# Sixteen of the 22 k-tiles of an FFN output projection as seven products of quarters, with the weight sums made in scratch DRAM

## The chip, the core and the metric

The kernel runs on one core of one Trainium2 chip. A core has five engines, each with an instruction queue of its own: TensorE (PE, matmuls; its weight loads are listed as PEld), VectorE (DVE), ScalarE (ACT), GpSimd (POOL) and SyncE (SP, which here only issues transfers). Transfers run on 16 DMA engines; most are issued by SP, and those that add to what they write are issued by POOL. Matmuls write to PSUM, eight banks of 128 x 512 words; everything else works on SBUF. The metric is the device time of the whole program in microseconds: 1425.68 us before the change, the median of 3 runs (1422.99 to 1426.24).

## What is computed

A trunk of two layers on x (512 tokens x 1024), with 256 memory tokens. Each layer has a token mixer, cross-attention and a SwiGLU FFN, each followed by a residual and a layer norm. Cut to what matters here:

```python
D_MODEL, SEQ, DEPTH = 1024, 512, 2
D_FF = 2816                       # 22 k-tiles of 128

def swiglu(x, w_in, w_out):
    g, u = jnp.split(x @ w_in, 2, axis=-1)
    return (jax.nn.silu(g) * u) @ w_out

h = layer_norm(x, ln0_g, ln0_b)
for l in range(DEPTH):
    mix = hybrid_mixer(h, ...)
    h = layer_norm(DEEPNORM_ALPHA * h + mix, ln1_g[l], ln1_b[l])
    xa = memory_cross_attention(h, mem, w_xq[l], w_xkv[l], w_xo[l])
    h = layer_norm(DEEPNORM_ALPHA * h + xa, ln2_g[l], ln2_b[l])
    ff = swiglu(h, w_ffn_in[l], w_ffn_out[l])
    h = layer_norm(DEEPNORM_ALPHA * h + ff, ln3_g[l], ln3_b[l])
```

All data are float32.

## The kernel before

**Three matmuls for one.** A float32 operand is split into a high part, which ScalarE copies into the matmul's type (line 101), and a low part, which VectorE or POOL subtracts (line 102). A product is three matmuls: high x high, high x low, low x high (`mm3`, lines 138 to 141).

**Buffers.** A weight chunk of 128 x 1024 words (512 KB) is loaded by SP into one of four `raw` buffers, then split into one of four `ring` tiles or, if it has to stay, into a `block` (`wchunk`, lines 121 to 136; `split_quarter`, line 355). There are 15 blocks of 8 KB per partition for everything that is large. PSUM has four banks with the tag `acc`, two with `tr` and two with `cv`. A tile that is asked for waits until a buffer of its tag is free.

**Order.** The code is written as one program. A scheduler, working at compile time with a simulated timeline, takes for each engine the ready instruction that stands first in the program; blocks under `tc.high_priority` count as standing further ahead. What it chose is then fixed: on the chip each engine runs its list in that order and waits at semaphores.

**The stages of a layer.** Mixer, first output projection (`po_mo`), cross-attention (`xq`, `scores`, `attn_out`, output projection `po_xo`), layer norm, FFN (lines 914 to 934).

**The FFN's input.** `swiglu_seven` (line 385) makes two k-tiles of the FFN's hidden layer, a pair, from seven products of quarters instead of eight: the layer norm's output is held as four quarters and their sums (`Quads`, line 299); the sums of weight quarters are made by two VectorE additions (lines 397, 398) and two adding DMAs from POOL (`add_into`, line 295). Each product is 24 matmuls of 256 columns into a pair of banks X, W or Y. At the end of a pair VectorE multiplies the two 128 x 512 results (line 464) and splits them (line 465) into `ph` and `pl`. The first pair of each layer goes through `swiglu_plain` (line 361), eight products.

**The FFN's output.** The 22 k-tiles come in three parts of 8, 6 and 8. After each part `out_proj` (line 267) multiplies the hidden k-tiles (stationary) with rows of `w_ffn_out` (moving, 512 columns at a time) for the four token tiles, and VectorE adds each bank into the residual `h` (line 286). The last part also makes the layer norm of each token tile. Chunks 0 to 3 of the weights go into the ring, the others into blocks.

**Lines of the prediction besides these.** 482 (transposes of the memory tokens), 507, 516 and 517 (loads of x and of two rows of the first norm), 554 and 555 (POOL applies the first norm's gain and bias to h), 566 (load of the convolution's rows), 584 (POOL clears `attT` at the head of each layer), 172 (loads of a norm's gain and bias), 351 and 125 (loads of weights).

Of the kernel before, what the change touches and what calls it, by code (L numbers as in the profile page):

```python
# [20 lines left out]
P = 128  # L21
# [30 lines left out]
def trunk(ctx: ExitStack, tc, a, out):  # L52
# [20 lines left out]
    def block(shape, dt, name):  # L73
        return blk.tile(shape, dt, tag="b", name=name)
# [25 lines left out]
    def split(hi, lo, src, eng=DVE):  # L100
        ACT.activation(hi, src, AF.Copy)  # L101
        eng.tensor_sub(lo, src, f(hi))  # L102
# [191 lines left out]

    def add_into(dst, src):

        POOL.dma_start(dst, src, accum_op=ALU.add)  # L297

    class Quads:

# [57 lines left out]
        split(flat[:, 0], flat[:, 1], raw)  # L358
        return w

    def swiglu_plain(w, q, j, ph, pl, name):
# [13 lines left out]
        out = []  # L375
        with tc.high_priority(offset=HP):
            for m in range(2):
                sg = tmp.tile([P, T], F32, tag="t", name=f"sg{j}{m}_{name}")
                ACT.activation(sg, banks[0][m], AF.Silu)
                DVE.tensor_mul(sg, sg, banks[1][m])  # L380
                split(ph[:, m, :], pl[:, m, :], sg)
                out.append((ph[:, m, :], pl[:, m, :]))
        return out

    def swiglu_seven(w, q, j, ph, pl, i0, name):

# [22 lines left out]
        def product(wq, b, banks, start, stop):  # L409
            for m in range(2):  # L410
                ms = slice(m * P, (m + 1) * P)
                for k in range(4):
                    wh, wl, bh, bl = wq[:, 0, k, ms], wq[:, 1, k, ms], b[:, 0, k, :], b[:, 1, k, :]
                    o = banks[m][:, :256]
                    PE.matmul(o, wh, bh, start=start and k == 0, stop=False, skip_group_check=True)  # L415
                    PE.matmul(o, wh, bl, start=False, stop=False, skip_group_check=True)  # L416
                    PE.matmul(o, wl, bh, start=False, stop=stop and k == 3, skip_group_check=True)  # L417
# [36 lines left out]
        product(w3, q.b[1, 1], X, False, True)  # L454
        with tc.high_priority(offset=HP):
            for m in range(2):
                ACT.activation(sg[m][:, hi], X[m][:, lo], AF.Silu)
        product(w4, t4, W, False, True)
        out = []
        with tc.high_priority(offset=HP):  # L460
            for m in range(2):
                DVE.tensor_add(uu[m][:, lo], W[m][:, lo], u2[m])
            for m in range(2):
                DVE.scalar_tensor_tensor(sg[m], sg[m], -1.0, uu[m], ALU.mult, ALU.mult)
                split(ph[:, i0 + m, :], pl[:, i0 + m, :], sg[m])
                out.append((ph[:, i0 + m, :], pl[:, i0 + m, :]))
        return out


    def mem_T(name):  # L470
# [89 lines left out]
    for l in range(L):  # L560
# [324 lines left out]
        def attn_out(hd, PT):  # L885
            oh, ol = oT[hd // 2]
            for e in range(2):
                po = bank(n_(f"o{hd}{e}"), tag="cv" if hd == XH - 1 else "acc")
                es = slice(hd * 256 + e * P, hd * 256 + (e + 1) * P)
                for m in range(2):  # L890
                    mm3(po, V[0][:, m, es], V[1][:, m, es], PT[:, 0, m, :], PT[:, 1, m, :], m == 0, m == 1)
                i = (hd % 2) * 2 + e
                split(oh[:, i, :], ol[:, i, :], po)

        q0, q1 = xq((0, 1), halves=True)
# [16 lines left out]


        w_fi, w_fo = a["w_ffn_in"][l], a["w_ffn_out"][l]
        for part, (j0, nj) in enumerate(((0, 8), (8, 6), (14, 8))):
            pT = []
            for j in range(j0, j0 + nj, 2):
                if (j - j0) % 4 == 0:
                    ph = block([P, 4, T], F32R, n_(f"ph{j}"))
                    pl = block([P, 4, T], F32R, n_(f"pl{j}"))  # L920
                if j == 0:
                    pT += swiglu_plain(w_fi, quads, j, ph, pl, f"{l}")
                else:
                    pT += swiglu_seven(w_fi, quads, j, ph, pl, (j - j0) % 4, f"{l}")
            norm = None
            if part == 2:
                gb3 = load_gb(a["ln3_g"][l], a["ln3_b"][l], n_("ln3"))
                hT = new_hT(n_("ln3")) if l < L - 1 else None

                def norm(tt, st):  # L930
                    layer_norm(tt, st, gb3, n_("ln3"), hT,
                               store=out[0, tt * P:(tt + 1) * P, :] if l == L - 1 else None)
            out_proj(w_fo[j0 * P:(j0 + nj) * P, :], pT, n_(f"fo{part}"), ALPHA if part == 0 else 1.0, norm=norm,
                     fin=part == 2 and l == L - 1)


_NAMES = [
# [18 lines left out]
```

## Time and profile before

| | |
|---|---|
| median of 3 runs | 1425.68 us (1422.99 to 1426.24) |
| the profiled execution | 1427.96 us, its span from the first to the last instruction 1426.0 us |
| granted TensorE clock, mean | 0.996 |
| DMA | 168.63 MB, 118 GB/s on average |
| weight chunks of `w_ffn_out` | 44 loads of 512 KB by SP |
| adding DMAs | 40 of 512 KB by POOL, all SBUF to SBUF |
| first and last `po_fo` matmul of layer 0's three parts | 454.3 to 503.4, 558.3 to 596.5, 671.6 to 722.5 us |
| the same in layer 1 | 1150.1 to 1199.1, 1254.1 to 1292.3, 1367.4 to 1416.9 us |

The profile is one execution; times in it are counted from the first instruction. "Busy" is the time in which an engine has at least one instruction in work. TensorE's matmuls overlap, so their mean duration is longer than the distance from one to the next. The chain of work is followed back from the last instruction, at each step to what released it. A wait is put down to the event that came last before the instruction could start.

### The profile page before, as it was taken

What the parts mean: (1) busy time and instruction counts of PE and PEld (TensorE: products, weight loads), DVE (VectorE), ACT (ScalarE), POOL (GpSimd) and SP (SyncE); (2) the same over time, 40 slices, a digit from 0 to 9 for tenths busy, and PEclk for the clock granted to TensorE, in tenths of its full rate; (3) what the DMA queues carried; (4) which work ended last, traced back from release to release, by engine and by line L of the source; (5) the groups of instructions that cost most, each with busy time, mean ns of one, the idle gap of its engine ahead of it and who ended that gap; (6) DMA issues with size and microseconds to landing.
All of it is one profiled execution on the core that took longest, in us unless ns stands there. A gap on an engine that the chain in (4) does not pass through costs nothing.

```text
span 1426.0 us, 22119 instructions
## 1 busy us (share of the span) xinstructions
PE 1396.7 (98%) x8949; PEld 1251.3 (88%) x8949; DVE 1034.0 (73%) x1701; ACT 608.0 (43%) x977; POOL 151.4 (11%) x98
## 2 busy tenths in 40 slices
PE   7998989999999999999999999999999999999997
PEld 6787888988899899899897889889889998989996
DVE  6699978656886376576769999685678764756667
ACT  5552461442456055255136235524525632534540
POOL 2373330000010000000013200000000000000000
PEclk9999999999999999999999999999999999999999
DMA  7522242322265364465242235512215663545531
GB/s 253 152 63 90 86 151 71 105 70 92 75 163 148 104 155 126 122 167 155 77 124 89 74 114 168 163 59 89 78 42 142 165 181 75 137 144 134 163 104 60
DMA packets 109306, 168.63 MB, mean 118 GB/s; under 512 B 7548, under 2 KB 82000, under 8 KB 109204
## 3 DMA queue, kind: packets, MB, share of 16 engines
q1 hardware_dynamic: 103156, 145.99, 31.9%
q0 software_dynamic: 5760, 20.97, 7.8%
q8 instruction: 70, 1.15, 0.3%
q14 instruction: 32, 0.26, 0.1%
q10 hardware_dynamic: 288, 0.26, 0.1%
HBM read 144.13 MB, written 2.10 MB: 103 GB/s over the span
## 4 chain that ended last, share of the span: by engine, by line
PE 85%; DVE 6%; issue 3%; ACT 3%; POOL 2%; DMA 1%; SPq 0%; DVEq 0%; POOLq 0%; ACTq 0%
PE po_fo L140 6%; PE po_fo L139 6%; PE po_fo L141 6%; PE fx L417 5%; PE fx L415 5%; PE fx L416 5%; PE fw L416 3%; PE fw L417 3%; PE fw L415 3%; DVE cv L611 3%; PE pp_xq L139 2%; PE pp_xq L140 2%; PE pp_xq L141 2%; PE po_xo L141 2%; PE po_xo L139 2%
## 5 line engine op out<-in xcount | busy, mean ns | idle before, releaser
L611 DVE SCALAR_TENSOR_TENSOR cv<-u,chan,cv 128x511 f32<-128x511 f32 (+29 forms) x240 | 159.6, 728 | 0.2
L140 PE MATMUL po_fo<-w_fo,ph 128*128 128x512 f32 (+1 forms) x360 | 138.2, 385 | 0.0
L141 PE MATMUL po_fo<-w_fo,pl 128*128 128x512 f32 (+1 forms) x360 | 137.6, 385 | 0.0
L297 POOL DMA_DIRECT2D s<-raw_a x40 | 34.8, 873 | 952.9 <-PE pp_f L141 473.8
L139 PE MATMUL po_fo<-w_fo,ph 128*128 128x512 f32 (+1 forms) x360 | 132.0, 385 | 0.0
L101 ACT ACTIVATE w_a<-raw_a 128x1024 fp32r<-128x1024 f32 x60 | 63.2, 1055 | 135.6 <-PE po_fo L141 110.2
L102 DVE TENSOR_TENSOR w_s<-s,w_s 128x1024 fp32r<-128x1024 f32 x80 | 97.3, 1220 | 28.3 <-ACT w_s L101 28.1
L101 ACT ACTIVATE w_s<-s 128x1024 fp32r<-128x1024 f32 x80 | 83.8, 1053 | 46.6 <-DMA s<-raw_a 33.6
L286 DVE SCALAR_TENSOR_TENSOR h<-h,po_fo 128x512 f32<-128x512 f32 (+1 forms) x49 | 32.6, 674 | 90.6 <-PE po_fo L141 90.6
L417 PE MATMUL fx<-T_ln,w_s 128*128 128x256 f32 x320 | 90.6, 283 | 0.0
L416 PE MATMUL fx<-T_ln,w_s 128*128 128x256 f32 x320 | 90.6, 283 | 0.0
L415 PE MATMUL fx<-T_ln,w_s 128*128 128x256 f32 x320 | 90.6, 283 | 0.0
L102 DVE TENSOR_TENSOR w_a<-raw_a,w_a 128x1024 fp32r<-128x1024 f32 x60 | 73.2, 1220 | 11.7 <-ACT w_a L101 10.5
L141 PEld LDWEIGHTS po_fo<-w_fo,pl 128*128 128x128 f32 x360 | 67.7, 188 | 13.2
L140 PEld LDWEIGHTS po_fo<-w_fo,ph 128*128 128x128 f32 x360 | 67.7, 188 | 13.0
L139 PEld LDWEIGHTS po_fo<-w_fo,ph 128*128 128x128 f32 x360 | 67.3, 188 | 12.9
L102 DVE TENSOR_TENSOR w_fo<-raw_fo,w_fo 128x1024 fp32r<-128x1024 f32 x44 | 52.9, 1219 | 16.2 <-ACT w_fo L101 16.2
L415 PEld LDWEIGHTS fx<-T_ln,w_s 128*128 128x128 f32 x320 | 61.4, 192 | 0.0
L416 PEld LDWEIGHTS fx<-T_ln,w_s 128*128 128x128 f32 x320 | 61.4, 192 | 0.0
L417 PEld LDWEIGHTS fx<-T_ln,w_s 128*128 128x128 f32 x320 | 61.4, 192 | 0.0
L140 PE MATMUL pp_xq<-hT_ln,w_xq 128*128 128x256 f32 (+1 forms) x192 | 61.3, 322 | 0.0
L139 PE MATMUL pp_xq<-hT_ln,w_xq 128*128 128x256 f32 (+1 forms) x192 | 60.0, 320 | 0.5 <-ACT hT_ln L101 0.5
(317 smaller groups left out, 4420.5 us busy)
## 6 DMA issues: line engine op xcount, KB each, us to landing
raw_a<-w_ffn_in SPq DMA_DIRECT2D x60, 512.0 KB
raw_fo<-w_ffn_out SPq DMA_DIRECT2D x44, 512.0 KB
s<-raw_a POOLq DMA_DIRECT2D x40, 512.0 KB, 5.1
s<-w_ffn_in SPq DMA_DIRECT2D x20, 512.0 KB
raw_xv<-w_xkv SPq DMA_DIRECT2D x16, 512.0 KB
raw_c<-w_in SPq DMA_DIRECT2D x16, 512.0 KB
raw_xk<-w_xkv SPq DMA_DIRECT2D x16, 512.0 KB
raw_mo<-w_mix_out SPq DMA_DIRECT2D x16, 512.0 KB
```

The costliest lines, as they stand in the source:

```text
L101: ACT.activation(hi, src, AF.Copy)
L102: eng.tensor_sub(lo, src, f(hi))
L139: PE.matmul(o, lh, rh, start=start, stop=False)
L140: PE.matmul(o, lh, rl, start=False, stop=False)
L141: PE.matmul(o, ll, rh, start=False, stop=stop)
L286: DVE.scalar_tensor_tensor(h[tt][:, c0:c1], h[tt][:, c0:c1], scale, bks[c][:, :c1 - c0], ALU.mult, ALU.add)
L297: POOL.dma_start(dst, src, accum_op=ALU.add)
L415: PE.matmul(o, wh, bh, start=start and k == 0, stop=False, skip_group_check=True)
L416: PE.matmul(o, wh, bl, start=False, stop=False, skip_group_check=True)
L417: PE.matmul(o, wl, bh, start=False, stop=stop and k == 3, skip_group_check=True)
L611: DVE.scalar_tensor_tensor(cv[ct][:, s:], u[:, ct, :T - s], wj, cv[ct][:, s:], ALU.mult, ALU.add)
```

## The change

The parts are now of 8, 8 and 6 k-tiles. The output projections of the first two use `out_proj_seven`: the hidden tiles (2 halves of k by 2 halves of the tokens) and the weights (2 halves of k by 2 halves of the columns) are taken as quarters, and seven products of sums of quarters replace eight. k-tiles are paired even with odd, so each pair of the FFN's input gives one tile of each quarter. The sums of hidden quarters T1 to T4 are made by VectorE when a pair is ready (`PairQuads`), the sums of weight quarters S1 to S4 in scratch DRAM: SP copies a quarter there, and POOL adds the other terms by adding DMAs. The calls that issue these stand in the code of cross-attention, four steps (eight transfers) at a time. The third part stays with `out_proj`.

```diff
+    dram = ctx.enter_context(tc.tile_pool(name="dram", bufs=1, space=bass.MemoryType.DRAM))
...
-        POOL.dma_start(dst, src, accum_op=ALU.add)
+        POOL.dma_start(dst, src, accum_op=ALU.add, max_dma_last_dim=4096)
...
+    class PairQuads:
+        PLACE = {"11": (0, 4, 6, 10), "21": (1, 5, 7, 11), "22": (2, 3, 8, 9)}
+        SUMS = {"T1": 0, "T2": 1, "T4": 2, "T3": 3}
+
+        def __init__(self, j0, name):
+            self.j0 = j0
+            self.t = [block([P, 2, 4, 256], F32R, f"pT{i}_{name}") for i in range(4)]
+            self.b = [block([P, 2, 4, 256], F32R, f"pB{i}_{name}") for i in range(3)]
...
+        def second(self, j, sg, uu):
+            i = (j - self.j0) // 2
+            t3 = uu[1][:, 256:]
+            DVE.tensor_sub(t3, sg[1][:, 256:], sg[0][:, 256:])
+            split(*self.get("T3", i), t3)
+            split(*self.get("22", i), sg[1][:, 256:])
+
+        def first(self, j, sg, uu):
+            i = (j - self.j0) // 2
+            for m, n in enumerate(("11", "21")):
+                split(*self.get(n, i), sg[m][:, :256])
+            t1, t2, t4 = uu[0][:, :256], uu[0][:, 256:], uu[1][:, :256]
+            DVE.tensor_sub(t1, sg[0][:, :256], sg[0][:, 256:])
+            DVE.scalar_tensor_tensor(t2, t1, -1.0, sg[1][:, 256:], ALU.mult, ALU.subtract)
+            DVE.scalar_tensor_tensor(t4, t2, -1.0, sg[1][:, :256], ALU.mult, ALU.subtract)
+            split(self.t[i][:, 0, 0:2, :].rearrange("p e c -> p (e c)"),
+                  self.t[i][:, 1, 0:2, :].rearrange("p e c -> p (e c)"), uu[0])
+            split(*self.get("T4", i), t4)
+
+    def quarter_of(w, c, k, u):
+        v = w.rearrange("(q two p) c -> two p q c", two=2, p=P)
+        return v[k][:, 2 * u:2 * u + 2, c * 512:(c + 1) * 512]
+
+    def weight_sums(w, name):
+        s = {n: [dram.tile([P, 2, 512], F32, tag=f"{n}{u}_{name}", name=f"{n}{u}_{name}") for u in range(2)]
+             for n in ("S1", "S2", "S3", "S4")}
+        steps = []
+        for n, c, k in (("S3", 0, 0), ("S1", 1, 0), ("S2", 1, 1), ("S4", 0, 1)):
+            steps.append([lambda u=u, n=n, c=c, k=k: nc.sync.dma_start(s[n][u], quarter_of(w, c, k, u)) for u in range(2)])
+        for n, x in (("S3", (1, 0)), ("S1", (1, 1)), ("S2", "S3"), ("S4", "S2")):
+            steps.append([lambda u=u, n=n, x=x: add_into(s[n][u], s[x][u] if x in s else quarter_of(w, *x, u))
+                          for u in range(2)])
+        return s, steps
+
+    def out_proj_seven(w, sums, pq, name, scale):
...
+        def operand(n, u):
+            raw = stage.tile([P, 1024], F32, tag="raw", name=f"raw_{n}{u}_{name}")
+            src = sums[n][u] if n in sums else quarter_of(w, *A[n], u)
+            nc.sync.dma_start(raw.rearrange("p (k c) -> p k c", k=2), src)
+            wt = ring.tile([P, 2, 1024], F32R, tag="w", name=f"w_{n}{u}_{name}")
+            split(wt[:, 0, :], wt[:, 1, :], raw)
+            return wt
+
+        plan = (("S3", "T3", "W"), ("11", "11", "X"), ("12", "21", "Y"), ("S2", "T2", "X"), ("22", "T4", "W"),
+                ("S1", "T1", "X"), ("S4", "22", "X"))
+        tags = {"X": "acc", "W": "tr", "Y": "cv"}
...
+        def add(t, c, g, i):
...
+                DVE.scalar_tensor_tensor(h[tt][:, cs], h[tt][:, cs], k, banks[g][i], ALU.mult,
+                                         ALU.subtract if c else ALU.add)
...
+        for n, b, g in plan:
+            bank_major = n in ("S1", "S4")
+            parts = [(i, u) for i in range(2) for u in range(2)] if bank_major else \
+                [(i, u) for u in range(2) for i in range(2)]
+            for i, u in parts:
+                for k in range(2):
+                    ph, pl = pq.get(b, u * 2 + k)
...
+                    PE.matmul(o, ph[:, ts_], wh, start=first, stop=False, skip_group_check=True)
+                    PE.matmul(o, ph[:, ts_], wl, start=False, stop=False, skip_group_check=True)
+                    PE.matmul(o, pl[:, ts_], wh, start=False, stop=last, skip_group_check=True)
...
     def swiglu_seven(...)
...
+            if quads:
+                for m in range(2):
+                    DVE.scalar_tensor_tensor(sg[m][:, hi], sg[m][:, hi], -1.0, uu[m][:, hi], ALU.mult, ALU.mult)
+                dest.second(j, sg, uu)
         product(w4, t4, W, False, True)
...
-                DVE.scalar_tensor_tensor(sg[m], sg[m], -1.0, uu[m], ALU.mult, ALU.mult)
-                split(ph[:, i0 + m, :], pl[:, i0 + m, :], sg[m])
+                s = lo if quads else slice(0, T)
+                DVE.scalar_tensor_tensor(sg[m][:, s], sg[m][:, s], -1.0, uu[m][:, s], ALU.mult, ALU.mult)
+            dest.first(j, sg, uu)
...
+        sums = [weight_sums(a["w_ffn_out"][l][g * NK * P:(g + 1) * NK * P, :], n_(f"fs{g}")) for g in range(2)]
+        steps = [st for g in range(2) for st in sums[g][1]]
...
         q0, q1 = xq((0, 1), halves=True)
+        sum_step(4)
         pt0 = scores(0, q0)
         q2, = xq((2,))
+        sum_step(4)
         pt1 = scores(1, q1)
         attn_out(0, pt0)
+        sum_step(4)
         pt2 = scores(2, q2)
         q3, = xq((3,))
+        sum_step(4)
         pt3 = scores(3, q3)
...
-        for part, (j0, nj) in enumerate(((0, 8), (8, 6), (14, 8))):
+        for part, (j0, nj) in enumerate(((0, 8), (8, 8), (16, 6))):
+            seven = part < 2
+            p = PairQuads(j0, n_(f"p{part}")) if seven else Pairs(j0, nj, n_(f"p{part}"))
...
+            if seven:
+                out_proj_seven(w_part, sums[part][0], p, n_(f"fo{part}"), scale)
+                continue
```

Per layer that is 16 copies of 512 KB on SP's queue, 16 adding DMAs of 512 KB on POOL's, and 14 instead of 8 (or 6) weight chunks to load and split in each of the two projections.

More of the change, by code (lines that the diff above doesn't have):

```diff
@@ L374, in swiglu_plain @@
                                 kh == 0 and k == 0, kh == 1 and k == 3)
-        out = []
         with tc.high_priority(offset=HP):
+            sg, uu = ([tmp.tile([P, T], F32, tag="t", name=f"{s}{j}{m}_{name}") for m in range(2)] for s in ("sg", "uu"))
             for m in range(2):
[L378 to L382, printed above, removed]
@@ L383, in swiglu_plain, with __init__ @@
-        return out
-    def swiglu_seven(w, q, j, ph, pl, i0, name):
+                ACT.activation(sg[m], banks[0][m], AF.Silu)
+                DVE.tensor_mul(sg[m], sg[m], banks[1][m])
+            dest.second(j, sg, uu)
+            dest.first(j, sg, uu)
+    class Pairs:
+        def __init__(self, j0, nj, name):
+            self.j0 = j0
+            self.t = [[block([P, 4, T], F32R, f"p{j}{i}_{name}") for i in range(2)] for j in range(0, nj, 4)]
+            self.stat = [(self.t[i // 4][0][:, i % 4, :], self.t[i // 4][1][:, i % 4, :]) for i in range(nj)]
+        def second(self, j, sg, uu):
+            pass
+        def first(self, j, sg, uu):
+            for m in range(2):
+                split(*self.stat[j - self.j0 + m], sg[m])
@@ L389, in swiglu_seven @@
+    def swiglu_seven(w, q, j, dest, name):
         n = lambda s: f"{s}{j}_{name}"
@@ L457, in swiglu_seven @@
                 ACT.activation(sg[m][:, hi], X[m][:, lo], AF.Silu)
+            if quads:
+                for m in range(2):
+                    DVE.scalar_tensor_tensor(sg[m][:, hi], sg[m][:, hi], -1.0, uu[m][:, hi], ALU.mult, ALU.mult)
+                dest.second(j, sg, uu)
         product(w4, t4, W, False, True)
-        out = []
         with tc.high_priority(offset=HP):
@@ L914, in trunk, with norm @@
         w_fi, w_fo = a["w_ffn_in"][l], a["w_ffn_out"][l]
-        for part, (j0, nj) in enumerate(((0, 8), (8, 6), (14, 8))):
-            pT = []
+        for part, (j0, nj) in enumerate(((0, 8), (8, 8), (16, 6))):
+            seven = part < 2
+            p = PairQuads(j0, n_(f"p{part}")) if seven else Pairs(j0, nj, n_(f"p{part}"))
             for j in range(j0, j0 + nj, 2):
[L918 to L934, printed above, removed]
+                (swiglu_seven if j else swiglu_plain)(w_fi, quads, j, p, f"{l}")
+            scale = ALPHA if part == 0 else 1.0
+            w_part = w_fo[j0 * P:(j0 + nj) * P, :]
+            if seven:
+                out_proj_seven(w_part, sums[part][0], p, n_(f"fo{part}"), scale)
+                continue
+            gb3 = load_gb(a["ln3_g"][l], a["ln3_b"][l], n_("ln3"))
+            hT = new_hT(n_("ln3")) if l < L - 1 else None
+            def norm(tt, st):
+                layer_norm(tt, st, gb3, n_("ln3"), hT,
+                           store=out[0, tt * P:(tt + 1) * P, :] if l == L - 1 else None)
+            out_proj(w_part, p.stat, n_(f"fo{part}"), scale, norm=norm, fin=l == L - 1)
 _NAMES = [
```

42 lines of the change are left out of this document (39 added, 3 removed).

## The prediction

> **What bounds the kernel now.** I read the page's busy times and its chain of work first, then the windows, then rows of the timeline.
>
> ```profile
> span 1426.0 us, 22119 instructions
> PE 1396.7 (98%) x8949; PEld 1251.3 (88%) x8949; DVE 1034.0 (73%) x1701; ACT 608.0 (43%) x977; POOL 151.4 (11%) x98
> ...
> PE 85%; DVE 6%; issue 3%; ACT 3%; POOL 2%; DMA 1%; SPq 0%; DVEq 0%; POOLq 0%; ACTq 0%
> ```
>
> TensorE holds 85% of the chain that ended last. The windows say where it doesn't (columns: stretch, its length, busy time of PE, PEld, DVE, ACT and POOL with their instructions, granted clock, DMA share, GB/s):
>
> ```profile
> 0.00:10.00 10.00, 3.50 (x14) 2.95 (x15) 3.36 (x7) 3.63 (x5) 2.09 (x10) 1.00 0.77 259
> 10.00:39.00 29.00, 24.56 (x109) 19.36 (x109) 22.46 (x60) 18.30 (x22) 5.75 (x2) 1.00 0.66 232
> ...
> 255.00:374.00 119.00, 118.75 (x689) 104.17 (x688) 78.40 (x155) 44.63 (x85) 0.00 (x0) 1.00 0.24 78
> 374.00:454.00 80.00, 79.90 (x663) 79.27 (x662) 64.22 (x91) 44.63 (x72) 5.35 (x6) 1.00 0.55 146
> 454.00:504.00 50.00, 50.00 (x248) 42.46 (x247) 23.05 (x28) 13.19 (x16) 0.85 (x1) 1.00 0.41 122
> ```
>
> In layer 0 cross-attention runs from 255 to 374 us, and the FFN follows: products of its input projection to 454, then the output projection (`po_fo`) of the first part to 504. There TensorE has no gap at a granted clock of 1.00. The start is different: up to 39 us TensorE works 28 of 39 us, and the transfers are busy 0.77 and 0.66 of the time, the most of the whole span. A matmul that goes is therefore worth its full pace in the FFN, and DMA work that is harmless at 300 us isn't at 20 us.
>
> A busy matmul is not its pace, since matmuls overlap. The pace is the distance of starts, in rows of the timeline (start, duration):
>
> ```profile
> 484.10 0.39 PE L140 MATMUL po_fo<-w_fo,ph 128*128 128x512 f32 x1
> ...
> 490.22 0.39 PE L140 MATMUL po_fo<-w_fo,ph 128*128 128x512 f32 x1
> ...
> 442.77 0.28 PE L415 MATMUL fw<-T_ln,w_s 128*128 128x256 f32 x1
> ...
> 443.61 0.28 PE L416 MATMUL fw<-T_ln,w_s 128*128 128x256 f32 x1
> ```
>
> From 484.10 to 490.22 there are 27 steps: 0.2267 us per 512-wide matmul. From 442.77 to 443.61 there are 7: 0.120 us per 256-wide one.
>
> **What goes.** An output projection of 8 k-tiles takes 4 token tiles x 8 x 2 column halves x 3 = 192 matmuls of 512 columns. Seven products take 7 x 2 x 4 x 3 = 168. Two such parts in each of two layers save 4 x 24 = 96 matmuls; 8+8+6 k-tiles instead of 8+6+8 changes nothing else in the count but a few 256-wide matmuls of the last tile (under 0.1 us). 96 x 0.2267 = **21.8 us**. Nothing else is removed, so this is the most that can be gained.
>
> The Trainium skill's page "TensorE: Matmul & The Clock Gate", section "Back-to-back issue gap", gives a sustained spacing of about 131 ns for 512 columns beside the weight loads; by it the 96 would be worth 12.6 us. The trace disagrees with 226.7 ns, and the sum goes by the trace.
>
> **What is added to VectorE and ScalarE.** Durations (columns: shape, count, then total busy and mean ns):
>
> ```profile
> L102 DVE TENSOR_TENSOR w_s<-s,w_s 128x1024 fp32r<-128x1024 f32 x80 | 97.3, 1220 | 28.3 <-ACT w_s L101 28.1
> L102 DVE TENSOR_TENSOR pl<-sg,ph 128x512 fp32r<-128x512 f32 x44 | 30.1, 683 | 0.0
> L446 DVE TENSOR_TENSOR sg<-fy,x 128x256 f32<-128x256 f32 x40 | 16.8, 421 | 23.4 <-PE fy L417 23.4
> L286 DVE SCALAR_TENSOR_TENSOR h<-h,po_fo 128x512 f32<-128x512 f32 x47 | 31.8, 685 | 88.4 <-PE po_fo L141 88.4
> L101 ACT ACTIVATE w_fo<-raw_fo 128x1024 fp32r<-128x1024 f32 x44 | 45.9, 1054 | 18.0 <-DMA raw_fo<-w_ffn_out 15.7 <-PE fy L417 2.2
> ...
> 430.49 0.42 DVE L446 TENSOR_TENSOR sg<-fy,x 128x256 f32<-128x256 f32 x1
> 430.83 1.23 DVE L102 TENSOR_TENSOR w_a<-raw_a,w_a 128x1024 fp32r<-128x1024 f32 x1
> ```
>
> Per pair of k-tiles in the FFN's input, VectorE now does 9 x 1.22 (seven splits, two sums) + 6 x 0.42 + 4 x 0.683 = 16.2 us, against 7 products x 24 x 0.120 = 20.2 us of TensorE. The change replaces the last four instructions (2.7 us) by thirteen of 256 columns and one of 512 (13 x 0.42 + 0.68 = 6.1 us): 19.6 of 20.2 us. The last two rows, starts 0.34 us apart at a duration of 0.42, show that real occupancy is less. A seven-product output projection needs 14 weight splits and 14 adds into h: 14 x 1.22 + 14 x 0.685 = 26.7 us beside 168 x 0.2267 = 38.1 us of TensorE. A whole part: VectorE 4 x 19.6 + 26.7 = 105 of 4 x 20.2 + 38.1 = 119 us, 89%, before 65%. ScalarE gets 14 x 1.05 = 15 us in 38. Both fit on average, so I cost them at what isn't covered. (a) At the end of a pair VectorE's clump grows from 3.1 to 5.7 us. Four weight tiles in the ring are up to 4 x 2.88 = 11.5 us of products ahead, which hides it; I take 0.1 us in each of 16 pairs, 1.6 us. Uncovered it is 16 x 2.6 = 42 us; below nothing it can't be, as it adds work only. (b) The first product of each output projection needs T3 of the last pair, which is made one product (2.88 us) earlier; the second needs "11", made during the first (5.4 us): 0.5 us at each of four starts, 2 us; uncovered its nine short steps are 4 us each time. (c) Inside the projection each product holds two of four ring slots, so the product after next is split while the next runs: ACT 1.05 and DVE 2 x 1.22, 3.5 of 5.4 us: nothing. Its banks are read into h two products ahead of their next use, except S1 to S4, where the halves alternate: nothing.
>
> **What is added to the queues.** Per layer 16 copies of 512 KB from SP and 16 adds of 512 KB from POOL, DRAM to DRAM. The trace has neither; the nearest rows are plain loads (q1) and adds within SBUF (q0):
>
> ```profile
> q1 hardware_dynamic: 103156, 145.99, 31.9%
> q0 software_dynamic: 5760, 20.97, 7.8%
> s<-raw_a POOLq DMA_DIRECT2D x40, 512.0 KB, 5.1
> ...
> L297 POOL DMA_DIRECT2D s<-raw_a x40 | 34.8, 873 | 952.9 <-PE pp_f L141 473.8
> ...
> 212.59 44.75 SPq L125 DMA_DIRECT2D raw_xq<-w_xq  x8
> ```
>
> A load of 512 KB costs 0.319 x 1426 / 145.99 x 0.524 = 1.63 us of all 16 engines, an add 0.078 x 1426 / 20.97 x 0.524 = 2.78 us. I take 1.63 for a copy (bounds: 1.63, and 2.78 as it writes DRAM) and 2.78 for an add (to twice that, 5.6). In cross-attention that is 16 x 1.63 + 16 x 2.78 = 71 us, beside 0.24 x 119 = 29 us of loads, in 119 us: it fits, just. SP issued the eight loads of w_xq from 212.59 to 257 us, ahead of their use from 255 us on, so copies after the first four delay nobody as long as they come one by one between waits for buffers. On POOL an S2 add waits for S3 to land and S4 for S2; behind them stand the adds of the FFN, six in the stretch from 374 to 454 us, and ScalarE's splits wait for those. The 16 adds (5.1 us each to landing, in chains of three) are through by then. The new operand loads, 14 x 1.63 = 23 us in 38, come through the same four raw buffers. The cap of 4096 on an adding DMA's last dimension changes nothing for the adds that are there: 5760 packets for 40 of them are 144 each, about one per row of 4 KB. Cost if they run where they stand: nothing.
>
> Sum as placed: -21.8 + 1.6 + 2.0 = -18.2 us against the profiled execution's own 1427.96 us (span 1426.0): 1409.8. The median of the runs lies 2.3 us below that execution: 1407.5.
>
> **Where the copies really run.** A copy reads only an input and writes scratch with a tag of its own: it waits for no data and for no buffer. Nearly every load in the trace is held back by a buffer; nothing holds these but the order of the code.
>
> ```profile
> 1.03 0.95 POOL L584 MEMSET attT<- 128x1024 f32 x1
> 11.66 4.42 SPq L125 DMA_DIRECT2D raw_xv<-w_xkv  x4
> 57.74 0.50 SPq L172 DMA_DIRECT2D gb_ln<-ln_g  x1
> ...
> SPq L517 <- DMA raw_xv<-w_xkv: 1.0, 1, 1.0
> SPq L566 <- DVE y_ln L149: 8.6, 1, 8.6
> ...
> 79.24 7.07 POOL h L555 x3
> ```
>
> The clearing of `attT` stands at the head of the layer loop, yet it ran at 1.03 us, before nearly everything that stands above it: what is ready is moved up into an idle queue. SP was idle for 8.6 us ahead of line 566, with its last load before that at 11.66 to 16 us. So I expect the copies of both layers there, 32 x 1.63 = **52 us** of transfers (89 at 2.78) in front of `raw_c`, the weights of the first projection. How they hold the queue is seen in the wait on line 517: a load of a norm's row waits for a weight load that it doesn't use, the one eight transfers before it. SP has at most eight under way, and what stands behind 32 copies waits until 24 have landed. The engines are idle 0.34 x 29 = 10 us between 10 and 39 us; the rest, **42 us** (79), puts off the first projection. The adds follow the copies on POOL, which has work in the chain around 79 us; 32 issues at 0.873 us are 28 us, of which I take **12** (bounds 0, where POOL is idle, and 28). Below nothing this can't be, as TensorE needs `raw_c` to go on. The FFN keeps its -18.2.
>
> Forecast: 1407.5 + 42 + 12 = **1462 us**. Its own range: from 1430, if only half of the copies come first (16 x 1.63 - 10 = 16, and 6 on POOL), to 1507 (79 and 28 would give 1514; both at once are unlikely).
>
> **Rivals. A, the copies stay in cross-attention**, the other side of zero: 1407.5 us, with a range from 1403 (no cost at all: 1427.96 - 21.8 - 2.3 = 1403.9) to 1416. For it: SP didn't take every load that needs no data at once; the gain `gb_ln` of the first norm could have gone into the same 8.6 us, and went at 57.74 (but it needs one of the blocks, which are given out in turn). It decides at the number of copies ahead of `raw_c`: 18.2 + 10 us at 1.63 are 17 copies, so with fewer than that the kernel gets faster.
>
> **C, VectorE sets the pace** in the FFN, copies in place. A third of the uncovered 42 us: 1421 us. For it, 19.6 of 20.2 us; against, the overlap of its instructions.
>
> **D, the sums overrun cross-attention.** With adds at 5.6 us the DMA work is 144 us in 119; 25 us per layer spill into a stretch with 0.55 taken. If the loads lose half of that, 2 x 12 us: 1432 us at worst, 1420 likely. The Trainium skill, "DMA: Bandwidth & Descriptors", section "Issuing engines are not separate DMA queues", says that transfers issued by SP and POOL run on the same 16 engines and interleave; by that rule D follows once the sums are late. No row here shows long transfers of both at once.
>
> **How the numbers follow.** Forecast 0.52, A 0.34, C 0.08, D 0.06. The range must take in A and most of the forecast's own: 1403 to 1500. Within 0.2% (2.9 us, about what a measurement can tell from no change) means 1422.8 to 1428.5. Faster: A and half of C and D, 0.41. Same: 0.05, from C and D. Slower: the forecast and the rest, 0.54.
>
> **What would show it.** The forecast: copies on SP before the first `raw_c`, TensorE idle in the first 100 us, adds on POOL long before 255 us, and from cross-attention on a shorter kernel. A: the copies on SP after 210 us, the stages up to 255 us as they were, 96 fewer 512-wide matmuls and TensorE without gaps. C: TensorE waiting for weight splits in the FFN. D: those splits waiting for `raw` or `s` transfers after 374 us. The forecast is wrong if the stages before 255 us keep their length; the FFN's part of it, if 512-wide matmuls of the seven products start further apart than 0.227 us.

## The result and the profile after

The changed kernel takes 1545.24 us (median of 4 runs, 1542.88 to 1546.13), the kernel before 1425.96 us beside it: a ratio of 1.0835 (95% interval 1.0811 to 1.0859). It is slower by 119 us, where 36 had been forecast. The profiled execution took 1545.25 us. One execution of `spread2` below, the one that left its trace, ran at a granted clock of 0.753 and took 1687.21 us; it is left out.

The page of the changed kernel (busy times; slices of 38.6 us for TensorE, its granted clock and the transfers; the two queues; the chain of work that ended last; the group with the longest idle time of TensorE ahead of it):

```profile
span 1543.5 us, 22468 instructions
...
PE 1392.1 (90%) x8847; PEld 1241.4 (80%) x8847; DVE 1109.6 (72%) x1905; ACT 651.5 (42%) x1065; POOL 180.8 (12%) x130
...
PE   5370259999999999999999999999999999999997
...
PEclk8685579999999999999999999999999999999999
DMA  9996762251311555655652433361221555755741
...
q1 hardware_dynamic: 118388, 175.35, 35.0%
q0 software_dynamic: 12416, 37.75, 13.3%
...
PE 72%; DVE 9%; issue 8%; DMA 7%; ACT 2%; POOL 1%; SPq 0%; DVEq 0%; POOLq 0%; ACTq 0%
...
L142 PE MATMUL pp_c<-hT_ln,w_c 128*128 128x512 f32 (+1 forms) x160 | 57.7, 370 | 60.7 <-POOL w_c L103 60.7
```

TensorE works 4.6 us less than before, in a span that is 117.5 us longer. The loss lies in the first six slices (232 us): TensorE is busy 0 to 7 tenths there, at a clock of 0.5 to 0.8. From the seventh on it has hardly a gap, as before. One single wait is 60.7 us: matmuls of the first projection (`pp_c`) for a split that POOL makes.

The stages, from first and last starts in the views of the tiles (us; the kernels of the last five columns come below):

| stage | before | after | `no_sums` | `copies_only` | `pin_all` | `one_seven2` | `spread2_ring` |
|---|---|---|---|---|---|---|---|
| start to layer 0's first `pp_xq` | 254.9 | 383.1 | 252.6 | 285.6 | 253.6 | 255.6 | 254.1 |
| to layer 0's first `pp_f` (cross-attention) | 119.5 | 119.5 | 119.5 | 119.6 | 127.3 | 119.5 | 119.4 |
| to layer 0's last `po_fo` (FFN) | 348.1 | 339.9 | 337.5 | 339.0 | 341.2 | 343.9 | 340.5 |
| to layer 1's last `pp_c` (between the layers) | 53.7 | 58.8 | 58.2 | 58.2 | 58.1 | 53.7 | 57.8 |
| to layer 1's first `pp_f` (mixer, cross-attention) | 294.0 | 294.0 | 293.4 | 293.4 | 300.5 | 293.3 | 293.3 |
| to layer 1's last `po_fo` (FFN) | 346.7 | 337.8 | 337.9 | 338.7 | 337.3 | 343.4 | 340.6 |
| to the end | 9.1 | 10.4 | 10.4 | 10.5 | 10.5 | 8.8 | 10.4 |
| span | 1426.0 | 1543.5 | 1409.5 | 1445.0 | 1428.5 | 1418.2 | 1416.1 |

So the changed kernel is 128.2 us late when cross-attention begins. The two FFN parts win back 8.2 and 8.9 us; the stretch between the layers and the end lose 5.1 and 1.3.

SP's transfers in the timeline (start, length of the piece, line, what, how many): the first loads of `raw_c` in the kernel before, then the changed kernel.

```profile
27.31 9.67 SPq L125 DMA_DIRECT2D raw_c<-w_in  x4
```

```profile
12.54 4.38 SPq L452 DMA_DIRECT2D S_fs<-w_ffn_out  x4
...
23.54 29.01 SPq L452 DMA_DIRECT2D S_fs<-w_ffn_out  x14
...
65.49 5.74 SPq L452 DMA_DIRECT2D S_fs<-w_ffn_out  x6
71.33 0.56 SPq L126 DMA_DIRECT2D raw_c<-w_in  x1
...
103.05 8.62 SPq L126 DMA_DIRECT2D raw_c<-w_in  x3
```

This is the forecast's picture: 27 of the 32 copies are in front of the first projection's weights, and `raw_c` begins at 71.33 us instead of 27.31. But the chain, followed in order of time, goes on after the copies:

```profile
44.34 16.31 DMA S_fs<-w_ffn_out
60.67 8.72 DMA rows<-b_a
69.39 3.87 issue
...
94.05 7.80 issue
102.41 1.34 POOL S_fs L298
103.75 8.13 issue
...
174.33 2.38 POOL w_c L103
```

From 69 to 174 us it is made of adds on POOL (`S_fs` L298, about 1 us each) and of "issue" between them, time in which the engine waits for nothing that the profile shows. POOL's own timeline has the rows (in brackets the idle time ahead and its releaser):

```profile
20.83 1.23 POOL L298 DMA_DIRECT2D S_fs<-w_ffn_out  x1 [18.02 <-DMA S_fs<-w_ffn_out]
32.09 1.07 POOL L298 DMA_DIRECT2D S_fs<-w_ffn_out  x1 [10.04 <-issue]
42.19 1.04 POOL L298 DMA_DIRECT2D S_fs<-w_ffn_out  x1 [9.03 <-issue]
...
146.83 1.05 POOL L298 DMA_DIRECT2D S_fs<-w_ffn_out  x1 [5.12 <-issue]
153.03 1.04 POOL L298 DMA_DIRECT2D S_fs<-w_ffn_out  x1 [5.16 <-issue]
...
168.42 0.82 POOL L298 DMA_DIRECT2D S_fs<-S_fs  x1 [2.25 <-issue]
170.87 0.81 POOL L298 DMA_DIRECT2D S_fs<-S_fs  x1 [1.63 <-issue]
...
174.06 2.63 POOL L103 TENSOR_TENSOR w_c<-raw_c,w_c 128x1024 fp32r<-128x1024 f32 x1
```

26 of the 32 adds stand ahead of POOL's first split for `pp_c`. Where the source is `w_ffn_out` they are issued 9 to 11 us apart up to 120 us, beside the copies and the loads behind them, and 6 to 7 us apart later. The last ones, where source and target are scratch, are 2.5 to 3 us apart. The 26 go out between 20.83 and 173.5 us, and the split behind them waits. That wait, not the one for the copies, ended last.

### The profile page after: what moved, and what is told of

It is laid out like the page before. It is cut to its first block, busy times and chain, and to the rows that moved or that the text cites. A ratio compares the mean times of both kernels' runs of the same rounds, so it can differ in the third digit from the quotient of the medians.

```text
span 1543.5 us, 22468 instructions
## 1 busy us (share of the span) xinstructions
PE 1392.1 (90%) x8847; PEld 1241.4 (80%) x8847; DVE 1109.6 (72%) x1905; ACT 651.5 (42%) x1065; POOL 180.8 (12%) x130
## 4 chain that ended last, share of the span: by engine, by line
PE 72%; DVE 9%; issue 8%; DMA 7%; ACT 2%; POOL 1%; SPq 0%; DVEq 0%; POOLq 0%; ACTq 0%
PE fx L541 5%; PE fx L543 4%; PE fx L542 4%; DVE cv L740 4%; DMA S_fs<-w_ffn_out 3%; PE fw L541 2%; PE fw L543 2%; PE fw L542 2%; PE pp_xq L140 2%; PE pp_xq L141 2%; PE pp_xq L142 2%; PE po_mo L140 2%; PE po_mo L141 2%; PE po_mo L142 2%; PE po_xo L142 2%
## 5 line engine op out<-in xcount | busy, mean ns | idle before, releaser
L298 POOL DMA_DIRECT2D s<-raw_a x40 | 34.8, 896 | 959.1 <-PE pp_f L142 292.4
L142 PE MATMUL pp_c<-hT_ln,w_c 128*128 128x512 f32 (+1 forms) x160 | 57.7, 370 | 60.7 <-POOL w_c L103 60.7
L142 PEld LDWEIGHTS pp_c<-hT_ln,w_c 128*128 128x128 f32 x160 | 32.9, 206 | 66.1 <-POOL w_c L103 61.1
L140 PE MATMUL pp_c<-hT_ln,w_c 128*128 128x512 f32 (+1 forms) x160 | 59.3, 376 | 23.8 <-ACT w_c L102 21.8
L775 DVE TENSOR_TENSOR qk<-qk 128x1024 f32<-128x1024 f32 x2 | 14.8, 7403 | 68.6 <-ACT qk L774 68.6
L141 PE MATMUL pp_xq<-hT_ln,w_xq 128*128 128x256 f32 (+1 forms) x192 | 61.2, 322 | 0.0
L140 PE MATMUL pp_xq<-hT_ln,w_xq 128*128 128x256 f32 (+1 forms) x192 | 60.1, 321 | 0.5 <-ACT hT_ln L102 0.5
L142 PE MATMUL pp_xq<-hT_ln,w_xq 128*128 128x256 f32 (+1 forms) x192 | 60.4, 318 | 0.0
L141 PE MATMUL pp_c<-hT_ln,w_c 128*128 128x512 f32 (+1 forms) x160 | 59.1, 371 | 0.2 <-DVE hT_ln L103 0.2
L102 ACT ACTIVATE hT_ln<-lt_ln 128x512 fp32r<-128x512 f32 x24 | 13.6, 595 | 103.1 <-PE lt_ln L207 103.0
L140 PEld LDWEIGHTS pp_c<-hT_ln,w_c 128*128 128x128 f32 x160 | 32.5, 205 | 29.8 <-ACT w_c L102 22.7
```

Source lines behind the costliest of these rows:

```text
L140: PE.matmul(o, lh, rh, start=start, stop=False)
L141: PE.matmul(o, lh, rl, start=False, stop=False)
L142: PE.matmul(o, ll, rh, start=False, stop=stop)
L298: POOL.dma_start(dst, src, accum_op=ALU.add, max_dma_last_dim=4096)
L775: DVE.tensor_add(nl, nl, ab)
```

## The experiments

Two theories stood against each other for the 128 us at the start. The first: POOL's queue is held, as each add goes out only some time after the one before, and POOL's splits stand behind. The second: the transfers themselves fill the 16 engines and the weights come late. For the gain a third question: is it the forecast's 18.2 us?

**`pin_all`**: the sums are kept where the code has them, behind the work that stands ahead of them in the program (parts of the changed lines).

```diff
-   ... nc.sync.dma_start(s[n][u], quarter_of(w, c, k, u)) ...
+   ... tc.keep_in_program_order(nc.sync.dma_start(s[n][u], quarter_of(w, c, k, u))) ...
...
-   ... add_into(s[n][u], ...) ...
+   ... tc.keep_in_program_order(add_into(s[n][u], ...)) ...
```

> The 32 copies and 32 adds are kept behind the work that stands ahead of them in the program, so that they run in cross-attention. If the 119 us come from the sums' place at the start: the +128 us that cross-attention starts later in the changed kernel go, the feed-forward part keeps its gain, and the time is the forecast's sum as placed, 1407 us (1404 to 1415). If the sums cost the same wherever they run (their transfers or their issue time are the price): 1480 us or more, with TensorE idle inside cross-attention. If they overrun cross-attention's end: 1415 to 1432, with TensorE idle at the first product of the projection.

1430.85 us (ratio 1.0032, 1.002 to 1.0043). The place is worth 114 us, so the start was the cause. But the sum as placed, 1407, does not come out either: 23 us are missing, and the kernel is even a little slower than before. The time lies in the third range, without its sign: TensorE idles inside cross-attention. Cross-attention is longer by 7.8 us in layer 0 and by 7.2 in layer 1 (126.7 against 119.5, in the same views). SP's rows of `pin_all`, then the window from 290 to 310 us of `pin_all` and of the kernel before (columns as in the prediction):

```profile
251.63 1.51 SPq L126 DMA_DIRECT2D raw_xq<-w_xq  x2
253.20 16.15 SPq L452 DMA_DIRECT2D S_fs<-w_ffn_out  x8
269.44 8.84 SPq L126 DMA_DIRECT2D raw_xq<-w_xq  x2
```

```profile
290.00:310.00 20.00, 15.81 (x75) 13.53 (x76) 11.62 (x26) 9.33 (x23) 4.59 (x5) 0.83 0.88 200
```

```profile
290.00:310.00 20.00, 20.00 (x121) 17.73 (x120) 12.05 (x25) 8.32 (x22) 0.00 (x0) 1.00 0.16 53
```

Eight copies in a row, issued in 16.15 us, stand ahead of the last two loads of `w_xq`. In the waits of `pin_all` from 285 to 330 us the longest in total is that of a split of these weights:

```profile
ACT w_xq L102 <- DMA raw_xq<-w_xq: 11.4, 2, 10.4
```

TensorE works 15.81 of 20 us where it had no gap, and its granted clock is 0.83. No run tells the order on SP's queue from the full engines here (their busy share is 0.99 and 1.05 in the 40 us before this window).

**`no_sums`**: the steps that issue copies and adds are cleared, and the summed operands are read from a quarter.

```diff
-   src = sums[n][u] if n in sums else quarter_of(w, *A[n], u)
+   src = quarter_of(w, *A.get(n, (1, 0)), u)
```

> No copies and no adds: the four summed operands are read from a quarter of the weights itself, so the output is not the reference's. It gives what the seven products with their sums of activations are worth alone. By the forecast: 1407 us (1404 without any clump on VectorE). By the traces of the changed kernel, where the two feed-forward parts came out 8.2 and 8.9 us shorter: 1408 to 1410. If VectorE sets the pace of the pairs instead: 1421.

1413.70 us (0.9908, 0.9893 to 0.9923): 12.6 us faster. None of the three figures is met. In the profiles the FFN stages give 10.6 + 8.8 = 19.4 us of the 21.8 that 96 matmuls are worth; the stretch between the layers and the end give back 4.5 and 1.3. (The profiled executions of the two kernels lie 16.7 us apart, 4 more than the medians, 2.3 of it ahead of cross-attention.)

**`copies_only`** (the add steps are empty) and **`pin_adds`** (the second edge of `pin_all` alone):

> The copies float to the start as in the changed kernel, the 32 adds are left out (the operands are read from the copies alone, so the output is not the reference's). If POOL's queue, where each add waits for the one before while the splits of the first weights stand behind, is what holds the start: most of the loss goes, to 1440 to 1455 us (32 copies of 1.63 us, 10 of them hidden, as the forecast had them). If the transfers ahead of the first weights are the price: 1480 to 1500 us.

> The copies float to the start, the adds are kept behind the work ahead of them in the program, so that they run in cross-attention. If the adds cost at the start by blocking POOL and by their transfers there, and nothing in cross-attention: as with the copies alone, 1446 us (1442 to 1450). If the adds hold up cross-attention as well, as copies and adds pinned there together did by 15 us over the kernel without sums: 1455 to 1465.

1445.57 us (1.0133, 1.0102 to 1.0164) and 1448.11 us (1.0155, 1.0134 to 1.0177). Both are in the first range of their expectation. They don't tell the held queue from the adds' transfers, as both go with the adds. Copies at the start cost 1445.57 - 1413.70 = 31.9 us. Moving the adds alone to cross-attention takes away 97 of the 119 us. SP's rows of `copies_only`:

```profile
23.63 21.65 SPq L452 DMA_DIRECT2D S_fs<-w_ffn_out  x14
...
61.49 0.63 SPq L126 DMA_DIRECT2D raw_c<-w_in  x1
...
84.86 2.67 SPq L126 DMA_DIRECT2D raw_c<-w_in  x3
```

The first `raw_c` is 10 us earlier than in the changed kernel, and the last ones start at 84.86 instead of 103.05: the adds' transfers slow the copies as well.

**`free_pool`** and its control **`free_copies`** (the same without adds): VectorE makes layer 0's splits up to and with the value projection, and the residual.

```diff
-    wlo_engines(DVE, POOL)
+    wlo_engines(DVE)
...
-            POOL.tensor_mul(h[tt], h[tt], gb[:, 0, :])
-            POOL.tensor_add(h[tt], h[tt], gb[:, 1, :])
+            DVE.tensor_mul(h[tt], h[tt], gb[:, 0, :])
+            DVE.tensor_add(h[tt], h[tt], gb[:, 1, :])
...
-        wlo_engines(POOL)
+        wlo_engines(DVE if l == 0 else POOL)
```

> Copies and adds float as in the changed kernel, but the splits of the first weights and the residual of the first layer norm are VectorE's instead of POOL's, so that nothing of the start stands behind an add. If POOL's blocked queue is the cause: TensorE's work from the first projection on starts 60 to 90 us earlier and the time is 1455 to 1490 us. If the adds cost by their transfers (32 times 2.78 us at the least): 1530 to 1550 us, as in the changed kernel.

> The control of the run in which VectorE took POOL's work at the start: the same kernel with the adds left out, so the copies float and VectorE makes the first splits (the output is not the reference's). The difference between the two is what the adds cost at the start when nothing stands behind them on POOL. If VectorE's extra work costs nothing: 1446 us as with the copies alone, and the adds' transfers cost 48 us. If VectorE's extra work is most of those 48 us: 1480 us or more, and the transfers cost under 15.

1493.60 us (1.0469, 1.0451 to 1.0486) and 1457.49 us (1.0216, 1.0203 to 1.0229). With nothing behind the adds, 51.6 us are gone, although VectorE's extra work costs 1457.49 - 1445.57 = 11.9. The time is 3.6 us above the first theory's range. The adds still cost 1493.60 - 1457.49 = 36.1 us, put down here to their transfers. Of the 99.7 us that the adds cost at the start (1545.24 - 1445.57), 63.6 are then the held queue, if VectorE's extra work costs the same with adds and without. Both theories are right in part; the expected 1446 and 1480 of the control lie on either side of it. The waits of `free_pool` from 60 to 200 us show what comes next when POOL is out of the way (who waited for what: total, times, longest):

```profile
POOL S_fs L298 <- issue: 95.1, 21, 10.5
ACT w_c L102 <- DMA raw_c<-w_in: 53.0, 4, 34.3
```

POOL waits between its adds as long as in the changed kernel (94.1 us there), and it hurts nobody; ScalarE waits 53.0 us for `raw_c`, 38.1 in `free_copies`.

**`scratch`**: one number of the changed kernel, the descriptor memory of POOL's transfers, and the same order of instructions.

```diff
-    nc = _bacc.Bacc("TRN2", ..., dynamic_dma_scratch_size=1024)
+    nc = _bacc.Bacc("TRN2", ..., dynamic_dma_scratch_size=1536)
```

> The changed kernel with one number changed: the memory in which POOL's transfers keep their descriptors is 1536 bytes a partition instead of 1024; every instruction stands in the same order. If an add is issued 6 to 10 us after the one before because their descriptors don't fit together: two are under way at once, the adds' pitch on POOL falls to about a half, and the time to 1490 to 1520 us. If an add waits for the transfer before it or for a copy to land, or if the transfers themselves are the bound: 1540 to 1550 us and the same pitch.

1537.05 us (1.0776, 1.0753 to 1.0798): 8 us less, between the two ranges. But POOL's timeline shows why the adds had waited:

```profile
20.54 1.22 POOL L298 DMA_DIRECT2D S_fs<-w_ffn_out  x1 [17.74 <-DMA S_fs<-w_ffn_out]
22.23 1.05 POOL L298 DMA_DIRECT2D S_fs<-w_ffn_out  x1 [0.47 <-DMA S_fs<-w_ffn_out]
31.93 1.06 POOL L298 DMA_DIRECT2D S_fs<-w_ffn_out  x1 [8.66 <-issue]
36.19 1.04 POOL L298 DMA_DIRECT2D S_fs<-w_ffn_out  x1 [3.20 <-issue]
...
133.07 0.82 POOL L298 DMA_DIRECT2D S_fs<-S_fs  x1 [2.03 <-issue]
153.27 2.40 POOL L103 TENSOR_TENSOR w_c<-raw_c,w_c 128x1024 fp32r<-128x1024 f32 x1 [19.38 <-ACT w_c L102]
```

SP's timeline of `scratch` and its waits from 60 to 200 us have these rows:

```profile
88.61 5.56 SPq L126 DMA_DIRECT2D raw_c<-w_in  x1
...
ACT w_c L102 <- DMA raw_c<-w_in: 88.6, 5, 48.9
```

Adds that went one at a time now go in pairs, the last one ahead of the first `w_c` split is out at 133 us instead of 173.5, and POOL's idle time put down to "issue" falls from 94.1 to 39.7 us. So the descriptor memory set most of the pitch. The time hardly follows, because adds that go out sooner take their transfers sooner: `raw_c` is later still (88.61 us, 71.33 in the changed kernel), the split's operand is ready at 153 us only, and ScalarE's wait for `raw_c` is 88.6 us, 22.6 in the changed kernel. The queue and the transfers lie over each other, and where one is lifted the other shows. The 63.6 and 36.1 us above are therefore what comes off when the queue is freed first; in another order the shares would differ.

The packets of q0, the queue of the adding DMAs, fit to it. Before, 5760 for 40 adds are 144 each, 9 for each of 16 engines. The 6656 more of the changed kernel leave 272, 17 for each engine, for an add from `w_ffn_out` with its rows of 2 KB, if a scratch add with rows of 4 KB has 144 as well (16 x 144 + 16 x 272 = 6656). The Trainium skill, "DMA: Bandwidth & Descriptors", sections "Terms" and "The descriptor swizzle", says that a descriptor has 16 bytes, and that a transfer of 1 MiB to 128 partitions takes 9 to read and 9 to write on each engine, one of either to complete it. An estimate from that page, if both sides share the memory: 2 x 17 x 16 = 544 bytes, so that two of the larger adds don't fit into 1024 and do fit into 1536, and three of 2 x 9 x 16 = 288 fit into 1024. The trace agrees: one by one, in pairs, and the scratch adds 2.5 to 3 us apart where the median to landing is 7.7 us. No run shows that both sides share the memory; with one for each, three of the larger adds would fit (3 x 272 = 816 bytes), and the trace would not agree.

**`one_seven2`** asks where 6 of the 19.4 us went: without sums, one seven-product part, and a last part of eight k-tiles.

```diff
-        for part, (j0, nj) in enumerate(((0, 8), (8, 8), (16, 6))):
-            seven = part < 2
+        for part, (j0, nj) in enumerate(((0, 8), (8, 6), (14, 8))):
+            seven = part < 1
```

A first try, `one_seven`, also gave the middle part the layer norm of the last one. It took 1429.62 us (1.0025, 1.0015 to 1.0034), which says nothing about the question.

> As without sums, but only the first eight k-tiles are seven products, and the last part has eight k-tiles as in the kernel before, instead of six (the summed operands are read from a quarter, so the output is not the reference's). If 5 us of the gain are lost because the layer norms of a six-tile last part have less work of TensorE beside them: 1417 us (half of the 18.7 us that the feed-forward parts gain, and no loss at the layers' ends), with 3.8 us less between the layers than in the kernel without sums. If that loss has another cause: 1420 us (half of the whole gain of 12.6).

> As without sums, but only the first eight k-tiles are seven products, the middle part has six k-tiles and the last has eight, as in the kernel before; the layer norm stands behind the last part alone (in the run before this one the middle part had one as well). Summed operands are read from a quarter, so the output is not the reference's. If 5 us of the gain are lost because a last part of six tiles leaves TensorE less work beside the layer norms: 1417 us, with 54.4 us between the layers instead of 58.2. If that loss has another cause: 1420 us.

1418.64 us (0.9944, 0.9932 to 0.9956), between the two. The stages decide: 53.7 us between the layers, the kernel before's own figure (53.7 and not the expectation's 54.4), and 8.8 us at the end, no loss in either. The first 20 us after layer 0's last `po_fo`, in the kernel before, in `no_sums` and in `one_seven2`:

```profile
722.00:742.00 20.00, 19.75 (x161) 19.12 (x160) 11.88 (x25) 5.42 (x9) 0.40 (x1) 1.00 0.57 157
```

```profile
710.00:730.00 20.00, 18.05 (x135) 17.23 (x134) 15.95 (x35) 5.16 (x9) 0.00 (x0) 0.91 0.42 114
```

```profile
719.00:739.00 20.00, 19.75 (x164) 19.23 (x163) 11.39 (x24) 5.92 (x9) 0.89 (x1) 1.00 0.62 174
```

With eight k-tiles in the last part, TensorE's matmuls cover most of VectorE's layer norms, and VectorE has 11 to 12 us of work in the 20 behind them. With six (6 x 6 x 0.2267 = 8.2 us of matmuls for a token tile instead of 10.9) VectorE has 15.95 us left, TensorE has a gap of 2 us, and the granted clock is 0.91. The second seven-product part, with the two k-tiles that it takes from the last part, is worth 12.6 - 8.2 = 4.4 us of its 10.9, give or take some 3 by the two intervals.

**`spread`, `spread2`, `spread2_ring`** are meant to be faster. The copies are kept, two at a time, between the weight loads of the mixer, the adds behind the mixer's splits on POOL (the edit of `spread`).

```diff
+        def copy_step():
+            for st in copies_.pop(0):
+                st()
...
             mem_K(l, mT, KT, pr)
+            copy_step()
...
-        sum_step(4)
+        sum_step()
```

> A version meant to be faster: each layer's 16 copies are kept two by two between the weight loads of the mixer from the value projection on (so that no more than two stand ahead of a weight), and the 16 adds are kept behind the mixer's splits on POOL and run through cross-attention. If the 17 us between the pinned sums and none come from copies queued ahead of the weights of cross-attention: 1414 to 1419 us, 0.5 to 0.8% faster than before. If they come from the adds' transfers or their blocked queue: 1425 to 1432, no gain.

> As spread, but layer 1's copies come earlier, from its first projection on, so that its copies and adds are through before the weights of its mixer's output projection load. In spread these weights came late in layer 1 (po_mo and its layer norm took 54.0 us instead of 46.1). If that was the rest of the loss: 1410 to 1414 us, level with the kernel without sums. If the sums only move their cost to the layer's start: 1417 us or more.

> As spread2, with 1536 instead of 1024 bytes a partition for the descriptors of POOL's transfers. With the adds off the path, two of them under way at once should change nothing: within 3 us of spread2. If the adds' pitch still holds something up: 3 to 6 us faster than spread2.

1417.61 us (0.9944, 0.9925 to 0.9963), then 1417.32 (five runs, 0.9937, 0.9925 to 0.995), then 1415.94 us (0.9923, 0.991 to 0.9936). The three can't be told apart: earlier copies in layer 1 and more descriptor memory win nothing that is measured. `spread2` missed its 1410 to 1414, although the place named was mended, as the windows of `spread` and of `spread2_ring`, which has the same order, from 900 to 920 us show:

```profile
900.00:920.00 20.00, 15.12 (x60) 12.35 (x61) 12.44 (x27) 10.25 (x14) 0.00 (x0) 0.83 0.60 197
```

```profile
900.00:920.00 20.00, 20.00 (x94) 16.66 (x93) 16.17 (x36) 7.93 (x11) 0.00 (x0) 1.00 0.55 178
```

What is left against `no_sums` is 3.0 and 2.7 us in the two FFN parts (table). In layer 0 TensorE idles 2.0 us of its part instead of 0.5, and its 2375 matmuls, as many as in `no_sums`, are busy 338.5 us instead of 337.0; why stays open. All three are faster than both kernels, by 0.6 to 0.8% against the one before.

## Why the prediction was wrong

The direction and the first mechanism were right, the size was not. Its three terms, with what each measured (they sum to 36 and to 119 us). The first two miss by 5.6 and 10.1 us to opposite sides, so that nearly the whole error is the third's:

| term | forecast | measured | by |
|---|---|---|---|
| gain of the FFN with its costs | -18.2 | -12.6 | `no_sums` |
| copies ahead of `raw_c` | +42 | +31.9 | `copies_only` |
| adds on POOL | +12 | +99.7 | the changed kernel against `copies_only` |

**The step that failed** is "32 issues at 0.873 us are 28 us, of which I take 12". The duration of an issue was nearly right (about 1 us in POOL's rows), but it was taken for the time that an add holds the queue. An add goes out only some time after the one before, mostly by the descriptor memory as `scratch` shows, and POOL's splits behind the adds waited; that cost 63.6 us. The upper bound of 28 us was therefore no bound. A row that stood in the prediction had a better one: 5.1 us to landing for an adding DMA. One at a time, 32 of them are 163 us, and a range with that end would have reached past the result. The same step left out a second term: it counted the transfers of the copies at the start and not those of the adds that follow them, 32 x 2.78 = 89 us by its own price, of which 36.1 showed.

**The copies** moved as forecast and for the reason given. Their price of 1.63 us is near what was measured: q1, the queue of SP's transfers, took 0.350 x 1543.5 - 0.319 x 1426.0 = 85.3 us more for 32 copies and 24 more operand loads, 1.52 us each. How that divides is not settled: by the 48.3 us that the 24 loads add in `no_sums` (q1 there 35.7% of 1409.5 us) a copy is 1.16 us, and 1.71 in `copies_only` (38.6% of 1445.0). An add costs 0.133 x 1543.5 - 0.078 x 1426.0 = 94.1 us by 32, 2.94 us, close to the 2.78 taken. Of 32 x 1.52 = 48.6 us of copies 31.9 showed, so that some 17 were hidden and not 10.

**The FFN.** The pace of the new matmuls is what was forecast, in the timeline of the changed kernel:

```profile
603.53 0.39 PE L503 MATMUL foY_fo<-w_fo,pB_p 128*128 128x512 f32 x1
...
606.48 0.39 PE L502 MATMUL foX_fo<-w_S_fo,pT_p 128*128 128x512 f32 x1
```

13 steps in 2.95 us, 0.227 us each. The clumps and starts, 3.6 us in the forecast, came out at 21.8 - 19.4 = 2.4 or somewhat more, as the two FFN stages of `no_sums` have 56 and 53 matmuls fewer and not 48 each: some have moved behind the stages' ends. **Rival C** is out: in layer 0's whole FFN part, TensorE's waits in the changed kernel are these.

```profile
PE foX_fo L502 <- DVE h L485: 0.5, 2, 0.3
PE fx L541 <- ACT u L554: 0.4, 1, 0.4
PE fx L541 <- ACT w_a L102: 0.3, 1, 0.3
```

What the sum missed is in the sentence that 8+8+6 k-tiles instead of 8+6+8 "changes nothing else in the count". The count is right, but the last part covers the layer norms, and with its two k-tiles went 4.5 + 1.3 = 5.8 us of that cover. (The 89% of VectorE in the same working is 105 of 119 us, 88%; nothing rests on it.)

**Rival A** would have been wrong too: the copies in their place give 1430.85, not 1407.5. Its ground was that copies delay nobody "as long as they come one by one". They come eight in a row, ahead of the last two loads of `w_xq`. **Rival D**'s adds that overrun are not the reason: the last add of `pin_all` in layer 0 goes out at 312.8 us, 68 us ahead of the FFN, and with the adds alone in cross-attention `pin_adds` takes 2.5 us more than `copies_only`, which the spread of either's runs doesn't tell from nothing.

## What to carry to other kernels

A transfer that waits for nothing has no place of its own: tie it to the work that it is meant to run beside, and put it between loads in ones and twos: here the two loads behind a row of eight copies went out 16 us after the two ahead of it, and two by two ahead of the stage the copies left its length as it was (119.4 us). Price an instruction that issues a transfer by how long it holds its queue, bounded by the time to landing and not by its own duration, and count every transfer of the moved step. When work that covers something else is made shorter, price what it covered.

## What the runs showed of the hardware

- Adding DMAs of 512 KB on POOL hold what stands behind them until they are out. At 1024 bytes of descriptor memory a partition those of 272 packets went out one at a time, 9 to 11 us apart beside copies and loads and 6 to 7 us later, and those of 144 packets 2.5 to 3 us apart (packets divided as above). At 1536 bytes the larger ones went in pairs, and the 26th add was out at 133 us instead of 173.5.
- DRAM-to-DRAM transfers of 512 KB took 1.2 to 1.7 us (copy, by the run it is worked out from) and 2.94 us (adding) of the 16 engines, about as much as a load and an add within SBUF in the kernel before (1.63 and 2.78).
- Behind gaps of TensorE the granted clock was often lower: 0.83 beside 4.2 us of idle time in 20 (`pin_all`), 0.91 beside 2 us in 20 (`no_sums`), and 0.66 where TensorE worked 32 of the 100 us from 100 to 200 us in the changed kernel. It isn't so everywhere: in the first 39 us of the kernel before TensorE idled 10.9 us at a clock of 1.00.
